# Low parts of the keys on both halves of the partitions: the second score pass on 128 rows instead of two times 64

## The chip, the cores and the metric

The kernel runs on one core of a Trainium2 chip. The metric is the device time of one execution in microseconds (us), as the median of several executions. The core's engines are named as the profile names them: PE (TensorE, matmul), PEld (its loading of the stationary operand), DVE (VectorE), ACT (ScalarE), POOL (GpSimd) and SP (SyncE). ACT and SP also issue the DMAs of this kernel, each from its own in-order queue.

## The reference, cut to what matters

One decoder layer on 1024 tokens of 1024 channels: a norm, one combined projection, an attention branch and a state space branch side by side, a gated sum of the two, an output projection, a norm and the residual. The change touches the attention branch alone, and of it the logits of the two softmax maps:

```python
q = q.reshape(b, s, ATT_HEADS, 2, ATT_QK_DIM)        # 8 heads, 2 maps, 64 channels
k = k.reshape(b, s, ATT_HEADS, 2, ATT_QK_DIM)
...
logits = jnp.einsum('bqhcd,bkhcd->bhcqk', q_i, k) * scale
logits = logits + bias[None, :, None]
logits = jnp.where(causal, logits, -jnp.inf)
p = jax.nn.softmax(logits, axis=-1)
a = p[:, :, 0] - lam * p[:, :, 1]
return jnp.einsum('bhqk,bkhe->bqhe', a, v)
```

## The kernel before

PE takes the operands in a 32-bit format that keeps fewer bits than float32, so each float32 value is held as the sum of a high part and a low part (`split`, L96), and a product of two such values is made in passes over PE that add up in one PSUM tile. A projection takes three passes per 128 rows of the contraction (`mm3`, L144: high by high, high by low, low by high).

The phases run one after the other: the norm and the transposed activations hTH and hTL, then eight heads of `attention(h)` (L253) with one `gates(h)` each, then `branch_att`, the state space branch, and the end. Inside a head:

- `proj_T` makes the queries (ps named pq) and keys (pk) of a head for 512 tokens at a time, channels on partitions: 24 matmuls of 512 columns each. The head has 2 x 64 channels, the two maps: map 0 on partitions 0 to 63 (`lo`), map 1 on 64 to 127 (`hi`).
- The queries go to qs. For map m, one half of the 128 partitions holds the high part of the queries and the other half the low part. So one pass over 128 rows against a key tile that holds the same 64 channels on both halves gives (high + low) times key.
- The keys' high part goes to kh in that doubled form: ACT writes each map on its own half (L274, L275), and two DMAs of 128 KB, issued from ACT's queue, copy it to the other half (L278, L279).
- The keys' low part, made by DVE (L276, L277), is held once: tile kl is [128, 1024], each map on its own half.
- `proj_N` makes values and output gates (ps named pv, 24 matmuls of 256 columns for each of 8 groups of tokens).
- `attend` (L310) then goes over eight blocks of 128 queries. For up to 512 keys at a time it makes the scores s of both maps in one tile of two PSUM banks: one pass per map over kh with 128 rows (L321), and one pass per map over kl with 64 rows (L323), which uses the rows 0 to 63 for map 0 and 64 to 127 for map 1. The key range is 256, 384 or 512 columns wide. DVE adds the bias near the diagonal (L328) and takes the maximum (L331), ACT takes the exponentials (L342), DVE combines the maps (L357, p), PE transposes p (L360, tile pta), ACT and DVE split it (L362 ah, L363 al), and PE multiplies by the values (L366, L367, tile po). Behind four blocks, the outputs are normed, gated and transposed (L305, tile pto).

The two passes of 64 rows:

```python
for m in range(2):
    nc.tensor.matmul(s[:, m, 0:wide], qs[:, m, qsl], kh[:, m, lo:lo + wide], start=True, stop=False)
for m in range(2):
    nc.tensor.matmul(s[:, m, 0:wide], qs[m * DK:(m + 1) * DK, m, qsl], kl[m * DK:(m + 1) * DK, lo:lo + wide], start=False, stop=True)
```

Every engine runs its own instructions in order. That order isn't that of the source: a scheduler lays it out when the program is built, from its own idea of what is ready when, and so weaves the projections of the next head, and the gates, between the steps of the blocks. A kernel with other instructions gets another order in that phase. The tiles qs, near, p, ah and al have two buffers; kh, kl, vv and gg have one, so a new head's keys are written only when the last score pass of the head before has read them. The PSUM pools have two buffers each: psp (pq, pk, pv, pg), pss (s, both banks) and pst (pta, po, pto).

## Time and profile before

| | us |
|---|---|
| median of 3 runs | 1942.09 |
| lowest and highest run | 1940.66, 1942.88 |
| span of the profiled execution | 1944.2 |
| PE busy in it | 1844.8 (95%) |
| DVE busy | 1181.2 (61%) |
| ACT busy | 863.2 (44%) |

The profiled execution's span is 2.1 us (0.1%) above the median of the runs; the profile gives no time around the span for this execution, so the sums are made against the span and carried over to the median as they are. A busy share is an average over phases with different limits. A PE record ends when the matmul's result is out, while the next one has long begun; what a matmul costs in a full stream is the distance from its start to the start of the next one, its slot, and the lines of time are read that way below.

### The profile page before, as it was taken

The numbers are of one execution on the slowest core, as the hardware profiler recorded it, in microseconds if no ns is written. First come the engines' busy times: TensorE is split into PE (matmuls) and PEld (weight loads), VectorE is DVE, ScalarE is ACT, GpSimd is POOL, SyncE is SP. The second block draws the span as 40 slices with busy tenths as digits, with TensorE's granted clock in tenths as the row PEclk, the third lists the DMA queues.
The fourth block names the chain that finished last, engine by engine and source line by source line (L and its number), as shares of the span: only waits on it lengthen the run. The fifth ranks groups of instructions, "written<-read, shape, count | busy, mean of one in ns | idle before, by whom it ended". The sixth has DMA issues, their size and how long they took to land. (4 is left out here: it accounts for less than half of the span.)

```text
span 1944.2 us, 27890 instructions
## 1 busy us (share of the span) xinstructions
PE 1844.8 (95%) x10249; PEld 1549.2 (80%) x10249; DVE 1181.2 (61%) x2782; ACT 863.2 (44%) x2135; POOL 136.3 (7%) x154
## 2 busy tenths in 40 slices
PE   6999999999999999999898989898989899999998
PEld 4888878788787878888787878787878777877786
DVE  5476575766758553347575767676767565545433
ACT  6454454544546342125445454545454444432221
POOL 1000000000000010001111111110101022000000
PEclk9999999999999999999999999999999999999999
DMA  6121121121111125513222222222222224753532
GB/s 197 45 68 55 42 58 49 53 60 53 49 47 55 33 90 197 159 49 81 63 66 65 66 66 67 70 64 68 65 71 62 65 49 146 233 178 137 177 109 70
DMA packets 219717, 165.14 MB, mean 85 GB/s; under 512 B 12220, under 2 KB 186654, under 8 KB 219582
## 3 DMA queue, kind: packets, MB, share of 16 engines
q1 hardware_dynamic: 169390, 117.21, 20.7%
q10 hardware_dynamic: 50192, 46.16, 8.2%
q8 instruction: 81, 1.33, 0.3%
q14 instruction: 54, 0.44, 0.1%
HBM read 129.63 MB, written 31.08 MB: 83 GB/s over the span
## 5 line engine op out<-in xcount | busy, mean ns | idle before, releaser
L150 PE MATMUL pz<-wzh,hTL 128*128 128x256 f32 (+1 forms) x512 | 151.4, 296 | 0.0
L150 PE MATMUL pz<-wzh,hTH 128*128 128x256 f32 (+1 forms) x512 | 149.1, 291 | 0.3 <-DVE dtr L539 0.3
L150 PE MATMUL pz<-wzl,hTH 128*128 128x256 f32 (+1 forms) x512 | 147.6, 288 | 0.0
L150 PE MATMUL pv<-wvl,hTH 128*128 128x256 f32 x512 | 145.3, 284 | 0.0
L150 PE MATMUL pv<-wvh,hTH 128*128 128x256 f32 x512 | 144.1, 281 | 0.3 <-DVE kl L277 0.3
L150 PE MATMUL pv<-wvh,hTL 128*128 128x256 f32 x512 | 144.3, 282 | 0.0
L586 ACT ACTIVATE mt<-mt,acs 128x128 f32<-128x128 f32 x256 | 85.5, 391 | 119.0 <-DMA mt<-arow_d 119.0
L331 DVE TENSOR_REDUCE ng<-s 128x2 f32<-128x1024 f32 (+2 forms) x96 | 90.9, 950 | 14.3 <-PE s L323 14.1
L580 POOL TENSOR_TENSOR v<-xb,dsk 128x256 f32<-128x256 f32 x64 | 51.2, 809 | 687.7 <-ACT xb L572 615.0
L150 PEld LDWEIGHTS pz<-wzh,hTH 128*128 128x128 f32 x512 | 97.1, 190 | 1.4 <-PE pz L150 0.5
L150 PEld LDWEIGHTS pv<-wvh,hTH 128*128 128x128 f32 x512 | 97.2, 190 | 1.2 <-PE pv L150 0.5
L150 PEld LDWEIGHTS pz<-wzl,hTH 128*128 128x128 f32 x512 | 97.0, 190 | 0.5
L150 PEld LDWEIGHTS pz<-wzh,hTL 128*128 128x128 f32 x512 | 96.7, 189 | 0.7
L150 PEld LDWEIGHTS pv<-wvl,hTH 128*128 128x128 f32 x512 | 97.0, 189 | 0.4
L150 PEld LDWEIGHTS pv<-wvh,hTL 128*128 128x128 f32 x512 | 96.2, 188 | 0.0
L513 DVE SCALAR_TENSOR_TENSOR xT<-ux,cw,xT 128x512 f32<-128x512 f32 x96 | 75.7, 789 | 21.3 <-ACT xT L511 19.9
L342 ACT ACTIVATE p<-s,ngm 128x512 f32<-128x512 f32 (+3 forms) x128 | 76.4, 609 | 25.6 <-DVE ngm L337 25.6
L607 PE MATMUL pd<-xdt,mt 128*128 128x64 f32 x512 | 66.6, 273 | 15.6 <-DVE st L605 9.6
L607 PEld LDWEIGHTS pd<-xdt,mt 128*128 128x128 f32 x512 | 62.4, 191 | 21.0 <-ACT mt L586 11.9
L288 DVE TENSOR_TENSOR vv<-pv,vv 128x128 fp32r<-128x128 f32 x64 | 18.7, 292 | 98.3 <-ACT vv L287 98.1
L366 PE MATMUL po<-vv,ah 128*128 128x256 f32 x288 | 74.7, 289 | 0.0
L367 PE MATMUL po<-vv,al 128*128 128x256 f32 x288 | 72.4, 284 | 0.0
(869 smaller groups left out, 5364.3 us busy)
## 6 DMA issues: line engine op xcount, KB each, us to landing
mt<-arow_d ACTq DMA_DIRECT2D x64, 256.0 KB, 5.3
sig_d<-gt ACTq DMA_DIRECT2D x32, 256.0 KB, 2.2
y_d<-yT ACTq DMA_DIRECT2D x32, 256.0 KB, 2.1
yT_l<-y_d SPq DMA_DIRECT2D x32, 256.0 KB, 5.2
xt<-in_x SPq DMA_DIRECT2D x8, 512.0 KB, 5.7
kh<-kh ACTq DMA_DIRECT2D x32, 128.0 KB, 2.3
o_d<-oT ACTq DMA_DIRECT2D x16, 256.0 KB, 2.0
oTl<-o_d SPq DMA_DIRECT2D x8, 512.0 KB, 6.2
```

Of the source, the lines that this page charges most:

```text
L150: nc.tensor.matmul(ps, a, b, start=(i == 0), stop=(i == n - 1))
L288: nc.vector.tensor_tensor(vv[:, t, DV:], ps[:, 0:DV], f32(vv[:, t, 0:DV]), op=ALU.subtract)
L331: nc.vector.tensor_reduce(ng, s[:, :, 0:width], axis=AX.X, op=ALU.max, negate=True)
L342: nc.scalar.activation(p[:, m, lo:lo + width], s[:, m, 0:width], AF.Exp, bias=neg[:, m:m + 1], accum_out=sums[:, i, m:m + 1])
L366: nc.tensor.matmul(po[:, 0:256], ah[:, k, :], vv[:, k, :], start=(k == 0), stop=False)
L367: nc.tensor.matmul(po[:, 0:256], al[:, k, :], vv[:, k, :], start=False, stop=(k == qb))
L513: nc.vector.scalar_tensor_tensor(out_h, u[:, j:j + 512], cw[:, j, ct:ct + 1], out_h, op0=ALU.mult, op1=ALU.add)
L580: nc.gpsimd.tensor_tensor(v4(v), v4(xb[:, 0:256]), b4(dsk[:, hs]), op=ALU.mult)
L586: nc.scalar.activation(mt[:, i, :], mt[:, i, :], AF.Relu, scale=-1.0, bias=acs[:, c, g * HG + i:g * HG + i + 1])
L607: nc.tensor.matmul(pd[:, 0, i * PH:(i + 1) * PH], mt[:, i, :], xdt[:, i * PH:(i + 1) * PH], start=True, stop=True)
```

## The change

The low part of the keys is now held like the high part, on both halves of the partitions. The tile kl becomes [128, 2, 1024], which adds 4 KB per partition to the pool of the attention phase. DVE writes each map on its own half as before, and two more DMAs of 128 KB per 512 tokens copy it to the other half, issued from ACT's queue behind those of kh. In `attend` the second pass of a map takes the same 128-row stationary operand qs as the first and kl with 128 rows; it follows its first pass directly, so the order of a group is kh and kl of map 0, then kh and kl of map 1. The product of the two low parts, which was left out before, is now in the sum. Comments and docstrings go too, which shifts nothing; lines L278 to L321 move down by one (the copies of kh are L279 and L280 now, the first pass L322), and from L323 on the numbers are those of before.

```diff
-        kl = work.tile([P, S], F32R, tag="kl", bufs=1, name=f"kl{h}")
+        kl = work.tile([P, 2, S], F32R, tag="kl", bufs=1, name=f"kl{h}")
...
-            nc.vector.tensor_tensor(kl[lo, sl], ps[lo], f32(kh[lo, 0, sl]), op=ALU.subtract)
-            nc.vector.tensor_tensor(kl[hi, sl], ps[hi], f32(kh[hi, 1, sl]), op=ALU.subtract)
-            nc.scalar.dma_start(f32(kh[hi, 0, sl]), f32(kh[lo, 0, sl]))
-            nc.scalar.dma_start(f32(kh[lo, 1, sl]), f32(kh[hi, 1, sl]))
+            nc.vector.tensor_tensor(kl[lo, 0, sl], ps[lo], f32(kh[lo, 0, sl]), op=ALU.subtract)
+            nc.vector.tensor_tensor(kl[hi, 1, sl], ps[hi], f32(kh[hi, 1, sl]), op=ALU.subtract)
+            for part in (kh, kl):
+                nc.scalar.dma_start(f32(part[hi, 0, sl]), f32(part[lo, 0, sl]))
+                nc.scalar.dma_start(f32(part[lo, 1, sl]), f32(part[hi, 1, sl]))
...
             for m in range(2):
                 nc.tensor.matmul(s[:, m, 0:wide], qs[:, m, qsl], kh[:, m, lo:lo + wide], start=True, stop=False)
-            for m in range(2):
-                nc.tensor.matmul(s[:, m, 0:wide], qs[m * DK:(m + 1) * DK, m, qsl], kl[m * DK:(m + 1) * DK, lo:lo + wide], start=False, stop=True)
+                nc.tensor.matmul(s[:, m, 0:wide], qs[:, m, qsl], kl[:, m, lo:lo + wide], start=False, stop=True)
```

The number of matmuls is the same, 192 passes over kh and 192 over kl; ACT gets 32 DMA issues more. The scheduler lays out the attention phase anew. From the last block of the last head on, the order of PE, DVE and ACT is the same as before, and on POOL and SP it is the same throughout. Three places show what moves.

PE, head 2 (counted from 0), block 2: the score passes of one tile s over 384 keys. L366 and L367 are of block 0's output, pg is of the gates. Before:

```order
1276 L321 MATMUL s_2_0_2621<-kh_2150,qs_2149 128x384
1277 L366 MATMUL po_0_2579<-vv_2152,ah_0_2572 128x256
1278 L321 MATMUL s_2_0_2621<-kh_2150,qs_2149 128x384
1279 L323 MATMUL s_2_0_2621<-kl_2151,qs_2149 128x384
1280 L367 MATMUL po_0_2579<-vv_2152,al_0_2573 128x256
1281 L323 MATMUL s_2_0_2621<-kl_2151,qs_2149 128x384
1282 L150 MATMUL pg_0_3016<-hTH,wm2h 128x512
```

The same tile in the changed kernel:

```order
1326 L322 MATMUL s_2_0_2633<-kh_2158,qs_2157 128x384
1327 L323 MATMUL s_2_0_2633<-kl_2159,qs_2157 128x384
1328 L322 MATMUL s_2_0_2633<-kh_2158,qs_2157 128x384
1329 L323 MATMUL s_2_0_2633<-kl_2159,qs_2157 128x384
1330 L150 MATMUL pg_0_3028<-hTL,wm2l 128x512
1331 L150 MATMUL pg_0_3028<-hTH,wm2h 128x512
```

Before, a full-array matmul stood between the two passes of 64 rows; now the four passes stand together, first and second pass of a map in turn. In the whole order before, 85 of the 96 pairs of 64-row passes stand next to each other and 11 are parted in this way (5 of 512 columns, 6 of 384).

ACT, head 2, blocks 6 and 7, where the keys of head 3 (ps pk_0) are read out of PSUM. Before:

```order
293 L274 ACTIVATE kh_3073<-pk_0_3129 64x512
294 L275 ACTIVATE kh_3073<-pk_0_3129 64x512
295 L278 DMA kh_3073<-kh_3073 64x512
296 L362 ACTIVATE ah_6_2875<-pta_6_0_2878 128x512
297 L362 ACTIVATE ah_6_2875<-pta_6_4_2886 128x384
298 L279 DMA kh_3073<-kh_3073 64x512
299 L342 ACTIVATE p_7_2929,sums_7_2930<-s_7_0_2912,ngm_7_2927 128x512 x2
300 L370 ACTIVATE sq_6_2908<-po_6_2892,rec_6_2871 128x128
301 L342 ACTIVATE p_7_2929,sums_7_2930<-s_7_512_2919,ngm_7_2927 128x512
302 L372 ACTIVATE sq_6_2908,sso_1_2724<-o_6_2907 128x128
303 L342 ACTIVATE p_7_2929,sums_7_2930<-s_7_512_2919,ngm_7_2927 128x512
```

In the changed kernel:

```order
311 L279 DMA kh_3085<-kh_3085 64x512
312 L280 DMA kh_3085<-kh_3085 64x512
313 L362 ACTIVATE ah_6_2887<-pta_6_0_2890 128x512
314 L362 ACTIVATE ah_6_2887<-pta_6_4_2898 128x384
315 L342 ACTIVATE p_7_2941,sums_7_2942<-s_7_0_2924,ngm_7_2939 128x512 x2
316 L370 ACTIVATE sq_6_2920<-po_6_2904,rec_6_2883 128x128
317 L342 ACTIVATE p_7_2941,sums_7_2942<-s_7_512_2931,ngm_7_2939 128x512
318 L372 ACTIVATE sq_6_2920,sso_1_2736<-o_6_2919 128x128
319 L342 ACTIVATE p_7_2941,sums_7_2942<-s_7_512_2931,ngm_7_2939 128x512
320 L279 DMA kl_3086<-kl_3086 64x512
321 L280 DMA kl_3086<-kl_3086 64x512
322 L269 ACTIVATE qs_3084<-pq_1_3174 64x512
```

The two new DMA issues stand behind the exponentials of block 7, and ahead of the reading of the next queries.

PE, head 1, block 7: the end of block 6's output (po) and the transposes of block 7 (pta). The matmuls pq_1 are the next head's queries. Before:

```order
1012 L366 MATMUL po_6_1969<-vv_1229,ah_6_1952 128x256
1013 L367 MATMUL po_6_1969<-vv_1229,al_6_1953 128x256
1014 L150 MATMUL pq_1_2237<-hTH,w_2l 128x512
1015 L150 MATMUL pq_1_2237<-hTH,w_2h 128x512
1016 L150 MATMUL pq_1_2237<-hTL,w_2h 128x512
1017 L150 MATMUL pq_1_2237<-hTH,w_2l 128x512
```

In the changed kernel:

```order
1057 L366 MATMUL po_6_1977<-vv_1233,ah_6_1960 128x256
1058 L367 MATMUL po_6_1977<-vv_1233,al_6_1961 128x256
1059 L360 MATMUL pta_7_0_2028<-cst,p_7_2014 128x128 x4
1060 L150 MATMUL pq_1_2247<-hTL,w_2h 128x512
1061 L150 MATMUL pq_1_2247<-hTH,w_2l 128x512
1062 L360 MATMUL pta_7_4_2036<-cst,p_7_2014 128x128 x4
```

Before, 18 matmuls of 512 columns stood between po_6 and pta_7; now pta_7 follows po_6 directly. Counted from the end of block 7's scores to its first transpose, 32 matmuls of 512 columns, 7 transposes and 14 matmuls of 256 columns stood between before, and 22, 7 and 14 now, and the same in heads 3 and 5 of the changed kernel; in the other heads between 24 and 33 of 512 columns stand there, before and now.

## Rows read from the trace of the kernel before

**Rows 1.** The head of the page and its first part: the span; busy time, share of the span and instructions of each engine.

```profile
span 1944.2 us, 27890 instructions
PE 1844.8 (95%) x10249; PEld 1549.2 (80%) x10249; DVE 1181.2 (61%) x2782; ACT 863.2 (44%) x2135; POOL 136.3 (7%) x154
```

**Rows 2.** Busy time of each engine in one stretch, from the first score pass to the end of the last head's scores: us; busy us (instructions) of PE, PEld, DVE, ACT, POOL; granted clock of PE as a share of full speed; DMA share; GB/s.

```profile
57.00:703.00 646.00, 641.09 (x3882) 531.99 (x3881) 419.07 (x1070) 318.07 (x944) 23.21 (x18) 1.00 0.18 51
```

**Rows 3.** Who waited for whom in that stretch, PE alone: us in total, times, longest.

```profile
PE pta L360 <- DVE p L357: 2.4, 3, 0.9
PE pto L305 <- DVE o L304: 2.2, 8, 0.4
```

**Rows 4.** Instructions of PE in order of time, a group of 512 columns and the projection behind it: start us, duration us, engine, line, operation, out<-in, rows*columns of the array, count (two records that overlap are merged to one).

```profile
283.59 0.62 PE L321 MATMUL s<-kh,qs 128*128 128x512 f32 x2
284.14 0.50 PE L323 MATMUL s<-kl,qs 64*128 64x512 f32 x2
284.57 0.50 PE L150 MATMUL pk<-hTL,w_3h 128*128 128x512 f32 x1
284.90 0.39 PE L150 MATMUL pk<-hTH,w_3l 128*128 128x512 f32 x1
285.13 0.40 PE L150 MATMUL pk<-hTH,w_3h 128*128 128x512 f32 x1
285.37 0.39 PE L150 MATMUL pk<-hTL,w_3h 128*128 128x512 f32 x1
285.60 0.40 PE L150 MATMUL pk<-hTH,w_3l 128*128 128x512 f32 x1
```

**Rows 5.** The same view, two groups of 256 columns one behind the other, with the matmuls around them.

```profile
140.18 0.28 PE L150 MATMUL pv<-wvh,hTL 128*128 128x256 f32 x1
140.30 0.40 PE L321 MATMUL s<-kh,qs 128*128 128x256 f32 x2
140.63 0.38 PE L323 MATMUL s<-kl,qs 64*128 64x256 f32 x2
140.94 0.50 PE L321 MATMUL s<-kh,qs 128*128 128x256 f32 x2
141.37 0.38 PE L323 MATMUL s<-kl,qs 64*128 64x256 f32 x2
141.69 0.39 PE L150 MATMUL pv<-wvh,hTH 128*128 128x256 f32 x1
141.91 0.28 PE L150 MATMUL pv<-wvl,hTH 128*128 128x256 f32 x1
```

**Rows 6.** The same view, a group of 384 columns whose pair stands together.

```profile
81.80 0.51 PE L321 MATMUL s<-kh,qs 128*128 128x384 f32 x2
82.24 0.44 PE L323 MATMUL s<-kl,qs 64*128 64x384 f32 x2
82.61 0.50 PE L150 MATMUL pg<-hTH,wm0l 128*128 128x512 f32 x1
82.95 0.39 PE L321 MATMUL s<-kh,qs 128*128 128x512 f32 x1
```

**Rows 7.** The same view, a group of 384 columns whose pair is parted: the place in head 2, block 2, of which the order stands above.

```profile
245.61 0.34 PE L321 MATMUL s<-kh,qs 128*128 128x384 f32 x1
245.88 0.44 PE L323 MATMUL s<-kl,qs 64*128 64x384 f32 x1
246.25 0.38 PE L367 MATMUL po<-vv,al 128*128 128x256 f32 x1
246.56 0.44 PE L323 MATMUL s<-kl,qs 64*128 64x384 f32 x1
246.93 0.50 PE L150 MATMUL pg<-hTH,wm2h 128*128 128x512 f32 x1
247.26 0.39 PE L150 MATMUL pg<-hTL,wm2h 128*128 128x512 f32 x1
```

**Rows 8.** Groups of instructions by line and shape: the 64-row passes; count, busy us, mean ns of one, idle time of PE just before them.

```profile
L323 PE MATMUL s<-kl,qs 64*128 64x512 f32 x96 | 26.4, 495 | 0.0
...
L323 PE MATMUL s<-kl,qs 64*128 64x256 f32 x64 | 12.3, 381 | 0.0
...
L323 PE MATMUL s<-kl,qs 64*128 64x384 f32 x32 | 9.7, 437 | 0.0
```

**Rows 9.** Line L279 alone, the second copy of kh: time of the issue on ACT's queue (ns: min/median/max), first and last start; and the time from issue to landing.

```profile
L279 ACTq DMA_DIRECT2D kh<-kh x16: 468/508/553, 41.3 to 638.6; - x16
...
DMA to landing us min/median/max: 2.2/2.3/3.7
```

**Rows 10.** Instructions of ACT in order of time, around the first keys of head 1: the last issue of the copies of kh.

```profile
121.16 0.50 ACTq L279 DMA_DIRECT2D kh<-kh  x1
```

**Rows 11.** Instructions of DVE in order of time, at the same place: the last write of the low parts kl.

```profile
123.25 0.69 DVE L277 TENSOR_TENSOR kl<-pk,kh 64x512 fp32r<-64x512 f32 x1
```

**Rows 12.** Instructions of PE in order of time, block 7 of head 3: its last 64-row pair and its first transposes.

```profile
368.13 0.50 PE L323 MATMUL s<-kl,qs 64*128 64x512 f32 x2
...
377.15 0.63 PE L360 MATMUL pta<-cst,p 128*128 128x128 f32 x4
```

**Rows 13.** Instructions of DVE in order of time, the same block: the first and the last step between those two.

```profile
368.68 0.70 DVE L328 TENSOR_TENSOR s<-s,near 128x512 f32<-128x512 f32 x1 [0.26 <-PE s L323]
...
376.25 0.75 DVE L357 SCALAR_TENSOR_TENSOR p<-p,nlam 128x512 f32<-128x512 f32 x1
```

## Prediction

> **What bounds the kernel now.** I read the page's first part, then the stretch in which the changed lines run, then the lines of time inside it. PE is busy for 95% of the span [rows 1]. Between 57 and 703 us, where all score passes run, it is busy for 641.1 of 646.0 us at full granted clock, with DVE at 419 and ACT at 318 [rows 2], and the waits that PE is charged with there are a few microseconds [rows 3]. So in this phase the kernel takes as long as PE's stream of matmuls is, and a microsecond taken off that stream is a microsecond of the kernel, as long as the softmax steps on DVE and ACT come in time. A busy share doesn't say whether the stream itself is dense; the starts do. In a plain stream a matmul of 512 columns starts 0.23 us after the last one (284.90 to 285.60 in three steps [rows 4]), one of 256 columns 0.12 us (140.18 to 140.30 [rows 5]); for 384 columns I take the middle, 0.175 us. These are the slots I count with.
>
> **Part 1, the 64-row pairs go.** A pair of 64-row passes does run side by side: two records of mean 495 ns [rows 8] cover 0.50 us together [rows 4]. But the starts around it show what it costs. Of 512 columns: from the first L321 at 283.59 to the second matmul behind the pair at 284.90 there are 1.31 us, in which two full passes and one projection matmul have 3 x 0.232 = 0.70; so the pair costs 0.61. Part of it lies in itself (284.14 to 284.57), part ahead of it and part in the next matmul, whose slot is 0.33 and not 0.23 [rows 4]. Two full 128-row passes cost 0.46: a saving of 0.15 each. Of 256 columns: 140.30 to 141.91 is 1.61 us for two pairs, four full passes and one projection matmul; less 5 x 0.118 that is 1.02, or 0.51 a pair, against 0.24: a saving of 0.27 [rows 5]. Of 384: 81.80 to 82.95 is 1.15, less 2 x 0.175 + 0.23 leaves 0.57 against 0.35: 0.22 [rows 6]. Where another matmul parts the pair, the price is paid twice: 245.61 to 247.26 is 1.65, less 0.175 + 0.12 + 0.23 leaves 1.12 against 0.35: 0.77 [rows 7].
> There are 48 pairs of 512, 32 of 256 and 16 of 384 columns (half of each count in [rows 8]), and the order parts 5 of 512 and 6 of 384. So 43 x 0.15 + 32 x 0.27 + 10 x 0.22 + 11 x 0.77 = 6.5 + 8.6 + 2.2 + 8.5 = **25.8 us** less. This is the largest term, and it holds if a pass over kl with 128 rows costs a slot like the pass over kh.
> Against this stands a rule: the Trainium skill, TensorEngine Tiling (Array Packing), section Overview, gives a contraction of 64 or less up to twice the speed when two such matmuls share the array; its section Tiling Modes adds that a change of the mode drains the engine. The trace agrees that the two share the array, and that the stream pays around them; by the first rule alone the change would lose what the rival "the pair was one pass" below works out.
>
> **Part 2, the new copies.** Two DMAs more for each of 16 half-heads. Their landing: a copy of kh lands 2.3 us (at most 3.7) after its issue [rows 9]. In head 1 the last low part is ready at 123.94 [rows 11], 2.3 us after the last issue of kh's copies ended [rows 10], so kl lands some 3 to 5 us behind kh. In the new order the first pass over kl stands 17 us of slots or more behind the projection of the first keys of its head (head 1: 17.4), so I cost the landing at 0. It would cost up to 2 us a head if the order left less than about 8.
> Their issue: 0.5 us each on ACT [rows 9], 32 of them, 16 us on an engine that is idle for half of the stretch [rows 2]. ACT waits there until DVE has written kl; behind it stand the reading of the next queries (L269) and, in the blocks, the split of the transposes (L362). Both ends: 0, where ACT would have waited anyway for the transposes, and 16 us, where each issue delays PE in full. I take 2 us, near the low end, since the transposes come behind DVE steps that the issue doesn't delay. DVE's own work stays as it was.
>
> **Part 3, the new order.** The handoffs from softmax to PE are where a shorter stream gives time back. Block 7 is the longest: in head 3 its scores end at 368.6 and its first transpose starts at 377.15, right behind the first half of p (377.0) [rows 12, 13]: the chain takes 8.4 us. In the new order heads 1, 3 and 5 have 22 x 0.232 + 7 x 0.12 + 14 x 0.12 = 7.6 us of slots there (0.12 for a transpose is an upper estimate: four together take 0.63 us [rows 12]), so PE waits about 1 us, or 3 where DVE and ACT have other work in between. The other heads have 8.0 to 9.3, where before there were 8.2 to 10.1. Nothing below 0 is to be expected in these three heads; elsewhere a reshuffle can also take away waits, of which there are a few now [rows 3]. Bounds: -3 and +10 us over the phase; I take **+4**.
> The wider kl takes 4 KB more per partition of a pool that ends with the phase: 0. From the last head's last block on the order is unchanged, so what follows just starts earlier: 0.
>
> **The sum.** 1944.2 - 25.8 + 0 + 2 + 4 = 1924.4 us for the profiled execution; the median of the runs is 2.1 us lower, so **1922 us**, 1.0% faster. Ends: 25.8 plus 3 of waits that go gives 1913; 25.8 less 10 and less a third of ACT's 16 gives about 1932.
>
> **The rivals.**
> *The handoffs take most of it.* PE is dense now because the stream is long enough to hide the softmax chains. If the other five heads wait as the three do, with 2 to 3 us in a head at two blocks, 12 to 16 us come back on top: 1934 to 1938. For it: the chain of block 7 had no room to spare in head 3 [rows 12, 13]. Against it: PE's waits on p are 2.4 us in all now, in three places [rows 3], and the other blocks' room is about as before.
> *The cost stays.* If the gaps around the pair come from the change of the key tile and not from the 64 rows, the new passes cost a full slot plus the same gaps: ahead of and behind the pair about 0.2 us are lost, and the pair's own stretch (0.43 for 512, 0.31 for 256) becomes 0.46 and 0.24. That gains about 1 us for the pairs that stand together and 4 for the parted ones, less 6 of parts 2 and 3: 1943, no change. Against it: L366 and L367 change operands at every step.
> *The pair was one pass.* If two 64-row passes cost the time of one, doubling it adds a slot per pair: 48 x 0.232 + 32 x 0.118 + 16 x 0.175 = 17.7 us, 1960. It is what a packed array suggests; the starts in [rows 4 to 6] speak against it.
> *ACT's queue becomes the bound (slower).* At 16 places ACT holds two issues, and waits for DVE's second kl before that; in head 1 that write came 1.5 us after the issues of kh were through [rows 10, 11]. With its 0.69 us and two issues that is up to 3.2 us in which exponentials and splits stand still. If all of it reaches PE: 16 x 3.2 = 51 us, less 26: 1967. It decides for slower from 26 / 16 = 1.6 us per half-head on. Against it: the scheduler put the issues behind the exponentials in heads 3, 5 and 7, and ACT idles half the time [rows 2].
>
> **How the numbers follow.** The forecast, PE's stream shrinks by what the pairs cost and some of it goes into waits, 1912 to 1932: 80%. Handoffs take most, 1932 to 1939: 9%. The cost stays, 1939 to 1945: 4%. ACT's queue: 5% (1946 and more); one pass: 2% (1960). The range of 8 in 10 reaches a little into the second case: **1911 to 1935**. About 0.2% (4 us) is what a measurement of this kernel can tell from no change; faster by more than that 89%, within 4%, slower 7%.
>
> **What would show it.** In the profile after: passes over kl with 128 rows that start 0.23, 0.175 and 0.12 us after the pass over kh, and the matmul behind a group in a normal slot, show part 1. Score passes that wait for a DMA of kl would show part 2 wrong. Waits of PE for p (L357) of 1 to 3 us ahead of block 7's transposes in heads 1, 3 and 5, in total some 4 us more than now, show part 3. ACT idle ahead of the new issues, followed by PE waiting for L342 or L362, would show the last rival. The phase from the first to the last score pass should end near 683 where it ends near 703 now. The prediction is wrong if the kl slots are longer than the kh slots, or if PE's waits in the phase rise by more than 10 us.

## The result, and the profile after

The changed kernel takes **1930.6 us** in the median of 4 runs (1928.73 to 1933.76), the kernel before beside it on the same chip 1942.49 us (4 runs, 1940.66 to 1946.22): a ratio of 0.9936, interval 0.9917 to 0.9954. It is faster by 11.9 us, where 20 were forecast. One execution of one kernel below, e_gdve, ran at a mean granted clock of 0.70 and is left out.

The head of the page after and the stretch from the first to the last score pass, to hold against [rows 1, 2]:

```profile
span 1929.4 us, 27946 instructions
PE 1828.1 (95%) x10249; PEld 1564.5 (81%) x10249; DVE 1183.5 (61%) x2782; ACT 862.4 (45%) x2135; POOL 136.3 (7%) x154
```

```profile
57.00:690.00 633.00, 619.61 (x3868) 543.68 (x3868) 417.66 (x1064) 316.12 (x943) 23.16 (x18) 0.99 0.21 59
```

PE's busy time in the phase fell by 21.5 us, from 641.1 to 619.6, but the phase shrank by 13 only: 13.4 of 633 us are idle now, where 4.9 of 646 were. The granted clock is no longer 1.00 throughout. Both are new.

The first matmul of the state space phase (tile pz) is the cleanest mark in the traces: what stands ahead of it holds all that the change touches. Before and after, PE in order of time:

```profile
832.15 0.30 PE L150 MATMUL pz<-wzh,hTH 128*128 128x288 f32 x1
```

```profile
821.53 0.30 PE L150 MATMUL pz<-wzh,hTH 128*128 128x288 f32 x1
```

So 10.6 us are won by there. The rest of the difference between two executions is not the change's: from that matmul to the first one of the output projection of that branch (tile pys) there are 825.4 us before and 819.2 after, with the same instructions in the same order, and from 813 to 825 us in the kernels below that keep that order. I compare kernels by this mark, and give the whole times beside it. Each mark is of one traced execution, and it also holds what moves ahead of the phase: the first score pass starts between 56.2 and 58.4 us in all kernels but e_zero (44.9) and e_plmem (54.6), so a microsecond or two of a difference can lie there. From the first to the last score pass there are 643.0 us before and 632.8 after, 10.2 less.

**The passes.** A group of 512 columns and the projection behind it, as in [rows 4], and the start of a group of 256 columns, as in [rows 5]:

```profile
279.38 0.39 PE L322 MATMUL s<-kh,qs 128*128 128x512 f32 x1
279.61 0.39 PE L323 MATMUL s<-kl,qs 128*128 128x512 f32 x1
279.85 0.39 PE L322 MATMUL s<-kh,qs 128*128 128x512 f32 x1
280.07 0.40 PE L323 MATMUL s<-kl,qs 128*128 128x512 f32 x1
280.31 0.40 PE L150 MATMUL pk<-hTL,w_3h 128*128 128x512 f32 x1
280.55 0.39 PE L150 MATMUL pk<-hTH,w_3l 128*128 128x512 f32 x1
```

```profile
138.70 0.28 PE L322 MATMUL s<-kh,qs 128*128 128x256 f32 x1
138.82 0.40 PE L323 MATMUL s<-kl,qs 128*128 128x256 f32 x2
```

Every start is one slot behind the last, 0.23 and 0.12 us, and the projection behind the group too; over the whole trace a pass over kl starts 0.232, 0.179 and 0.118 us (median) behind its pass over kh, for 512, 384 and 256 columns. The four passes and the matmul behind them take 280.55 - 279.38 = 1.17 us, where [rows 4] had 1.31 for the same work. This part came as forecast.

**The waits.** PE's waits up to the end of the last scores (57 to 692 us), as in [rows 3]:

```profile
PE pto L306 <- DVE o L305: 11.3, 8, 2.6
PE pta L360 <- DVE p L357: 1.3, 2, 0.8
```

The wait for p went down (2.4 to 1.3 us), the wait for o went from 2.2 to 11.3 us. Three of its eight places make most of it: heads 1, 3 and 5, at 212.19, 376.02 and 539.85 us. PE at the first of them, in order of time:

```profile
212.19 0.40 PE L150 MATMUL pk<-hTH,w_2h 128*128 128x512 f32 x1
215.15 0.30 PE L306 MATMUL pto<-cst,o 128*128 128x128 f32 x1 [2.57 <-DVE o L305]
...
217.13 0.63 PE L150 MATMUL pk<-hTL,w_2h 128*128 128x512 f32 x1
217.56 0.63 PE L150 MATMUL pk<-hTH,w_2l 128*128 128x512 f32 x1
...
218.82 0.39 PE L150 MATMUL pk<-hTH,w_2l 128*128 128x512 f32 x1
```

The same place before:

```profile
218.79 0.39 PE L150 MATMUL pk<-hTL,w_2h 128*128 128x512 f32 x1
219.41 0.50 PE L305 MATMUL pto<-cst,o 128*128 128x128 f32 x2 [0.23 <-DVE o L304]
```

Two losses follow each other. The slot ahead of pto is 2.96 us, against 0.62 before. Then matmuls of 512 columns start 0.43 us apart, not 0.23, until 218.82. Busy time by stretch (the columns of [rows 2]) shows why:

```profile
212.20:215.20 3.00, 0.43 (x3) 0.08 (x2) 2.81 (x9) 0.00 (x0) 0.37 (x1) 1.00 0.62 166
215.20:218.60 3.40, 3.40 (x11) 2.68 (x12) 0.59 (x3) 0.69 (x1) 0.00 (x0) 0.53 0.03 11
```

The granted clock is 0.53 in the 3.4 us behind the gap: the lower of its two levels, 1.2 instead of 2.4 GHz, for nearly all of it; in the next 3.4 us it is 0.97. It costs 3.4 x (1 - 0.53) = 1.6 us. The other two places read alike (0.53 and 0.54). So 3 x (2.96 - 0.62 + 1.6) = 11.8 us went there.

**Why o is late.** DVE at the first place. Between the sum of squares and o stand eleven small steps of the rsqrt (L115, L105, three times L107 to L109), of 0.16 us each:

```profile
208.96 0.17 DVE L115 TENSOR_SCALAR rsv_o<-sso 128x4 f32<-128x4 f32 x1 [0.47 <-ACT sq L372]
...
209.76 1.15 DVE L109 SCALAR_TENSOR_TENSOR rsy_o<-rst_o,rsy_o 128x4 f32<-128x4 f32 x1
...
211.34 1.25 DVE L109 SCALAR_TENSOR_TENSOR rsy_o<-rst_o,rsy_o 128x4 f32<-128x4 f32 x1
...
212.82 0.69 DVE L271 SCALAR_TENSOR_TENSOR qs<-pq,qs 64x512 fp32r<-64x512 f32 x1
...
213.73 0.69 DVE L272 SCALAR_TENSOR_TENSOR qs<-pq,qs 64x512 fp32r<-64x512 f32 x1
...
214.65 1.14 DVE L305 SCALAR_TENSOR_TENSOR o<-o,rsy_o,gg 128x128 f32<-128x128 f32 x4
```

The first step and o at the same place before:

```profile
216.73 0.17 DVE L115 TENSOR_SCALAR rsv_o<-sso 128x4 f32<-128x4 f32 x1 [0.47 <-ACT sq L372]
...
218.91 0.88 DVE L304 SCALAR_TENSOR_TENSOR o<-o,rsy_o,gg 128x128 f32<-128x128 f32 x3
```

From the first step to o there are 214.65 - 208.96 = 5.69 us; before it was 2.18. 1.4 us are the low parts of the next queries (L271, L272), which now stand among the steps. The other 2.1 are two small steps that took 1.15 and 1.25 us. At those times POOL, which splits the gates' weights, runs:

```profile
209.58 1.31 POOL L99 TENSOR_TENSOR wm2l<-wm2r,wm2h 128x512 fp32r<-128x512 f32 x1 [77.55 <-DVE rst_o L107]
211.27 1.30 POOL L99 TENSOR_TENSOR wm2l<-wm2r,wm2h 128x512 fp32r<-128x512 f32 x1 [0.38 <-ACT wm2h L98]
```

209.76 + 1.15 = 210.91 and 209.58 + 1.31 = 210.89; 211.34 + 1.25 = 212.59 and 211.27 + 1.30 = 212.57: each long step ends with POOL's instruction.

The Trainium skill, SBUF — State Buffer, section SBUF: two separate sides, calls the port pair that DVE and GpSimd share an exclusive lock: where a DVE step has two inputs in SBUF and a GpSimd instruction reads SBUF, whichever starts first has the pair for its whole instruction, and the other waits. The trace agrees, with these two pairs of ends: both steps read two tiles in SBUF. It shows the other side as well. Of the DVE steps that start while POOL subtracts or multiplies, those with one operand in PSUM take their usual time (qs<-pq, 4 of 4; v<-pd,v of the state space phase, 19 of 19), and those with both in SBUF are held until POOL is done (rsy_o<-rst_o,rsy_o, 7 of 7; xdt<-xb,dts of the state space phase, 24 of 24).

### The profile page after: what moved, and what is told of

It is laid out like the page before. It is cut to its first block, busy times and chain, and to the rows that moved or that the text cites. A ratio compares the mean times of both kernels' runs of the same rounds, so it can differ in the third digit from the quotient of the medians.

```text
span 1929.4 us, 27946 instructions
## 1 busy us (share of the span) xinstructions
PE 1828.1 (95%) x10249; PEld 1564.5 (81%) x10249; DVE 1183.5 (61%) x2782; ACT 862.4 (45%) x2135; POOL 136.3 (7%) x154
## 5 line engine op out<-in xcount | busy, mean ns | idle before, releaser
L331 DVE TENSOR_REDUCE ng<-s 128x2 f32<-128x1024 f32 (+2 forms) x96 | 91.3, 952 | 12.4 <-PE s L323 11.9
L366 PE MATMUL po<-vv,ah 128*128 128x256 f32 x288 | 74.8, 289 | 0.0
L367 PE MATMUL po<-vv,al 128*128 128x256 f32 x288 | 71.8, 282 | 0.0
```

The source lines that it names most:

```text
L331: nc.vector.tensor_reduce(ng, s[:, :, 0:width], axis=AX.X, op=ALU.max, negate=True)
L366: nc.tensor.matmul(po[:, 0:256], ah[:, k, :], vv[:, k, :], start=(k == 0), stop=False)
L367: nc.tensor.matmul(po[:, 0:256], al[:, k, :], vv[:, k, :], start=False, stop=(k == qb))
```

## The experiments

My theory: the passes save what was forecast, and the new order of the scheduler (the planner, below), which ACT's new DMAs bring about, puts o late in three heads. Its rivals: the DMAs themselves cost; any shorter stream of PE is given back at the handoffs; and, within the theory, that POOL's overlap alone makes the gap, or the steps of the queries alone. All twelve, with the kernel before and the change; the third column is the start of the first pz, the last PE's wait at pto from 57 to 700 us (total, longest; where the stream is shorter, this takes in one wait of 0.2 us from behind the last scores):

| kernel | median us | ratio to before [interval] | pz | wait at pto |
|---|---|---|---|---|
| before | 1942.49 | | 832.1 | 2.2, 0.4 |
| changed | 1930.60 | 0.9936 [0.9917, 0.9954] | 821.5 | 11.3, 2.6 |
| e_zero | 1923.44 | 0.9884 [0.9848, 0.9920] | 816.8 | 4.9, 2.4 |
| e_poolq | 1920.70 | 0.9882 [0.9848, 0.9916] | 808.9 | 3.0, 1.0 |
| e_bcopies | 1947.99 | 1.0020 [1.0001, 1.0039] | 836.3 | 10.8, 2.6 |
| e_grouped | 1931.06 | 0.9947 [0.9925, 0.9969] | 821.5 | 11.3, 2.6 |
| e_plmem | 1907.66 | 0.9826 [0.9808, 0.9845] | 805.4 | 5.2, 1.3 |
| e_gdve | 1911.74 | 0.9847 [0.9825, 0.9870] | | |
| e_gdve_again | 1911.57 | 0.9842 [0.9823, 0.9861] | 806.1 | 2.4, 0.4 |
| e_bpermap | 1990.65 | 1.0258 [1.0236, 1.0280] | 880.2 | 1.8, 0.3 |
| e_spq | 1920.06 | 0.9898 [0.9878, 0.9917] | 809.0 | 3.0, 1.0 |
| e_bgdve | 1932.80 | 0.9944 [0.9926, 0.9961] | 826.2 | 1.8, 0.5 |
| e_spq_gdve | 1913.28 | 0.9845 [0.9827, 0.9862] | 804.7 | 1.7, 0.5 |
| e_pool4 | 1926.76 | 0.9927 [0.9903, 0.9951] | 810.9 | 7.8, 1.5 |

### Without the order: the copies on another queue, or none

**e_poolq**, and later **e_spq** with `nc.sync` in the place of `nc.gpsimd`:

```diff
-            for part in (kh, kl):
-                nc.scalar.dma_start(f32(part[hi, 0, sl]), f32(part[lo, 0, sl]))
-                nc.scalar.dma_start(f32(part[lo, 1, sl]), f32(part[hi, 1, sl]))
+            for part, eng in ((kh, nc.scalar), (kl, nc.gpsimd)):
+                eng.dma_start(f32(part[hi, 0, sl]), f32(part[lo, 0, sl]))
+                eng.dma_start(f32(part[lo, 1, sl]), f32(part[hi, 1, sl]))
```

> The changed kernel with the copies of kl given by POOL's queue; those of kh stay with ScalarE. The computation is whole. The planner's order has no qs and no kl step among the rsqrt steps. Theory (order): 1917 to 1919, no gap of 2.6 us at pto. Rival (the copies' transfers cost, whoever gives them): 1928 to 1931. Rival (shorter TensorE work is given back at the handoffs anyway): about 1930.

> The changed kernel with the copies of kl given by SP's queue instead of ScalarE; everything is computed, and the order on the engines is that of the kernel whose kl copies POOL gave. Theory (the order of the rsqrt steps, set off by ScalarE's extra DMAs, is what the changed kernel lost): as there, no gap of 2.6 us at pto, 1918 to 1922, the first to last score pass at 620 us. Rival (POOL's giving of the DMAs happened to move POOL's splits out of the way): gaps at pto again, 1926 to 1931.

Both came as the theory has it, e_poolq 1.7 us above its range in the whole time: pz at 808.9 and 809.0 us, 23 us ahead of the kernel before and 12.5 ahead of the changed one, with every DMA still made. The planner gave both the order of the kernel before up to pz, instruction by instruction, on DVE and ACT, and on PE but for the score passes. The waits of e_spq, from 57 to 700 us:

```profile
PE pta L360 <- DVE p L357: 3.1, 4, 0.9
PE pto L306 <- DVE o L305: 3.0, 9, 1.0
```

The gaps are gone, and with them the lower clock (1.00 from 57 to 677 us). That the DMAs' transfers cost, and that the gain is given back in any case, are both out. What PE gives back at handoffs with the shorter stream is about 3 us: 23.1 of 26.

How ACT's issues led to it is seen in ACT's rows at the first place, the changed kernel first (the first issue of kl's copies, the sums of squares, L372, and behind them the high parts of the gates' weights, L98), then e_spq:

```profile
204.31 0.47 ACTq L279 DMA_DIRECT2D kl<-kl  x1
...
208.52 0.31 ACT L372 ACTIVATE sq<-o 128x128 f32<-128x128 f32 x1 [0.42 <-DVE o L371]
...
208.83 0.62 ACT L98 ACTIVATE wm2h<-wm2r 128x512 fp32r<-128x512 f32 x1
...
210.56 0.63 ACT L98 ACTIVATE wm2h<-wm2r 128x512 fp32r<-128x512 f32 x1
```

```profile
204.58 0.63 ACT L98 ACTIVATE wm2h<-wm2r 128x512 fp32r<-128x512 f32 x1 [2.15 <-PE pq L150]
...
207.29 0.63 ACT L98 ACTIVATE wm2h<-wm2r 128x512 fp32r<-128x512 f32 x1
...
209.47 0.31 ACT L372 ACTIVATE sq<-o 128x128 f32<-128x128 f32 x1 [0.42 <-DVE o L371]
```

POOL's split follows each L98. In e_spq both are done before the sums of squares are ready; in the changed kernel both come behind them, and so POOL runs just when DVE is at the rsqrt.

**e_zero**: no copies of kl at all. One tile for all heads, the other half of each map set to zero once:

```diff
+        kl = work.tile([P, 2, S], F32R, tag="kl", bufs=1, name="kl")
+        nc.vector.memset(f32(kl[64:128, 0, :]), 0.0)
+        nc.vector.memset(f32(kl[0:64, 1, :]), 0.0)
...
-            for part in (kh, kl):
-                nc.scalar.dma_start(f32(part[hi, 0, sl]), f32(part[lo, 0, sl]))
-                nc.scalar.dma_start(f32(part[lo, 1, sl]), f32(part[hi, 1, sl]))
+            nc.scalar.dma_start(f32(kh[hi, 0, sl]), f32(kh[lo, 0, sl]))
+            nc.scalar.dma_start(f32(kh[lo, 1, sl]), f32(kh[hi, 1, sl]))
```

> The changed kernel without the copies of the low parts: the second pass takes kl with 128 rows, but the other half of each map is zeroed once at the start and stays zero (so the product of low part with low part is left out, as in the kernel before). ScalarE gives no more DMAs than in the kernel before, and the planner returns to an order in which neither the qs step nor the kl step stands between the steps of an output block's rsqrt. Theory (the order costs some 14 us: three gaps of 2.6 us at pto and half the clock behind each): 24 to 26 us below the kernel before, about 1917 to 1919, no gap over 2 us at pto in heads 1, 3 and 5. Rival (whatever is faster on TensorE is given back at the handoffs): about 1930, like the changed kernel, with the gaps elsewhere. Rival (the DMAs cost): 1917 to 1919 here, but the kernel with the copies on another queue stays at 1925 to 1930.

Only half hit: pz at 816.8, 15.3 us ahead of before, not 24 to 26. My reading of its order was wrong for the start of the phase: its first score pass comes at 44.9 us, not 56.8, and PE waits there; and in the first head the queries' steps and two long small steps do stand in the rsqrt (5.55 us to o). The wait at the start:

```profile
PE s L320 <- DVE qs L270: 5.3, 1, 5.3
```

No gap stands in heads 1, 3 and 5. It is one more order with its own luck, and says little about copies.

### The order alone, and the passes alone

**e_bcopies**: the kernel before with the changed kernel's tile, copies and order, and still its 64-row passes.

```diff
-                nc.tensor.matmul(s[:, m, 0:wide], qs[:, m, qsl], kl[:, m, lo:lo + wide], start=False, stop=True)
+            for m in range(2):
+                nc.tensor.matmul(s[:, m, 0:wide], qs[m * DK:(m + 1) * DK, m, qsl], kl[m * DK:(m + 1) * DK, m, lo:lo + wide], start=False, stop=True)
```

> The kernel before, its pairs of 64 rows kept, with kl made as two maps and copied to the other half as in the change, the copies being read by nobody. It has the changed kernel's order of instructions on every engine, and its DMAs. Theory (order): the three gaps at pto in heads 1, 3 and 5 come here too, at up to 2.6 us each, with half the clock behind them: about 1953 to 1956. Since the stream of TensorE is longer by 0.77 us per pair here, part of a gap may be covered: down to 1947. Rival (the gaps come of the shorter TensorE work and not of the order): 1942 to 1944.

The three gaps came with the order, each 2.96 us from start to start as in the changed kernel, so they don't come of the shorter stream. But the kernel lost less than I expected: 4.2 us at pz, below my 5 to 14. Part of the reason is the clock. Behind the first gap and the second:

```profile
220.60:224.00 3.40, 3.40 (x22) 3.00 (x23) 0.59 (x3) 1.58 (x3) 0.00 (x0) 1.00 0.20 77
...
387.00:390.40 3.40, 3.40 (x11) 2.66 (x12) 0.59 (x3) 0.69 (x1) 0.00 (x0) 0.51 0.00 0
```

The same gap of 2.96 us is followed by full clock at the first place (and the third) and by half clock at the second. Three gaps, one fall of the clock and the smaller gap in head 6 (1.68 us) come to 3 x 2.34 + 1.6 + 1.06 = 9.7 us; 5.5 of it are given back elsewhere in this order: 1.6 by shorter waits for p (0.8 us, against 2.4 in [rows 3]), and about 2.6, by the prediction's prices, because it parts 7 of the pairs (1 of 512 columns, 3 of 384, 3 of 256) where the order before parts 11: (5 - 1) x 0.62 + (6 - 3) x 0.55 - 3 x 0.50. Where the rest lies I did not follow up.

With e_spq this makes a table of four, the pz mark: old order with 64 rows 832.1, old order with 128 rows 809.0, new order with 64 rows 836.3, new order with 128 rows 821.5. The passes are worth 23.1 us in the old order and 14.8 in the new; the order costs 4.2 us with the long passes and 12.5 with the short. The two parts don't simply add up, since the order also sets how many pairs are parted and where PE waits.

**e_bgdve** and **e_spq_gdve**: the same pair once more in a third order. In both, DVE makes the gates' splits; the second has the change with kl's copies from SP.

```diff
-        wg = load_cols(w_in, 0, OM + d * P, P, "wa", f"wm{d}", eng=nc.gpsimd)
+        wg = load_cols(w_in, 0, OM + d * P, P, "wa", f"wm{d}")
```

> Control: the kernel before with the gates' low parts worked out by VectorE instead of POOL; nothing of the change. Its order on TensorE and VectorE is that of the next kernel (two kl steps stand in the rsqrt of heads 1, 3 and 5). Theory (POOL's splits cost the kernel before little, since none of them met an rsqrt there): 1935 to 1943, and the state-space phase starts within 3 us of where it does in the kernel before, 832.1 us. Rival (POOL's splits hold up VectorE enough to matter with the long passes too): 1920 to 1930.

> The changed kernel with the copies of kl given by SP's queue and the gates' low parts worked out by VectorE; everything is computed. It differs from the control in the passes and the copies alone, so the difference of the two is what the passes are worth with no change of order: theory 21 to 26 us below the control by the start of the state-space phase (26.2 us of pairs removed, up to 5 us given back at handoffs). As a whole: 1908 to 1918, no half clock between 60 and 690 us. Rival (VectorE, busier by 0.7 us per split, becomes the one waited for): 1920 to 1928, PE's waits for p and o above 8 us together.

804.7 against 826.2: the passes are worth 21.5 us here, with the same order on DVE, ACT and POOL; 1.8 of it lie ahead of the first score pass (58.4 and 56.6 us), and from the first to the last pass it is 19.5, where e_spq has 22.6. This order parts only 5 pairs, all of 512 columns, so the prediction's prices give 22.5 for it; the 26.2 of the expectation holds for the old order at most.

The control gained 5.9 us by itself, more than the theory had (3) and less than the rival. Part of it is that order: 6 pairs of 384 columns fewer are parted, 3.3 us by the prediction's prices. Part is POOL, which held DVE up in the kernel before as well. DVE at head 3 of that kernel, two halves of p that take 0.75 us each when alone [rows 13], and POOL beside them:

```profile
293.94 2.47 DVE L357 SCALAR_TENSOR_TENSOR p<-p,nlam 128x512 f32<-128x512 f32 x2
```

```profile
294.58 1.28 POOL L99 TENSOR_TENSOR wm3l<-wm3r,wm3h 128x512 fp32r<-128x512 f32 x1 [78.47 <-ACT wm3h L98]
```

The second half is held for about 1 us, and PE waits 0.86 us for it; head 6 has the same. These are two of the three waits for p in [rows 3], and the control has none. The 5.9 us are not taken apart further.

**e_grouped** puts the second passes behind both first ones:

```diff
                 nc.tensor.matmul(s[:, m, 0:wide], qs[:, m, qsl], kh[:, m, lo:lo + wide], start=True, stop=False)
+            for m in range(2):
                 nc.tensor.matmul(s[:, m, 0:wide], qs[:, m, qsl], kl[:, m, lo:lo + wide], start=False, stop=True)
```

> The changed kernel with the passes of a block's scores in the order kh map 0, kh map 1, kl map 0, kl map 1 instead of map by map; all of 128 rows, the order on all other engines as in the change. If the gain of the passes is the row count alone: the same as the changed kernel, 1928 to 1933. If it is the change of the written bank that costs a part (each pass here goes to the other map's bank than the one ahead of it): slower by up to 85 times 0.1 us, 1939.

pz at 821.5, the same to 0.1 us: the map order, and with it the bank written, is worth nothing. The row count is all.

**e_bpermap** parts every pair of the kernel before:

```diff
             for m in range(2):
                 nc.tensor.matmul(s[:, m, 0:wide], qs[:, m, qsl], kh[:, m, lo:lo + wide], start=True, stop=False)
-            for m in range(2):
                 nc.tensor.matmul(s[:, m, 0:wide], qs[m * DK:(m + 1) * DK, m, qsl], kl[m * DK:(m + 1) * DK, m, lo:lo + wide], start=False, stop=True)
```

> The kernel before with its score passes map by map: kh map 0, kl map 0 (64 rows), kh map 1, kl map 1 (64 rows), so that no two passes of 64 rows follow each other; the copies are made as in the change and read by nobody, the order elsewhere is that of the kernel before. If a pass of 64 rows between passes of 128 costs as much as the parted pair of the kernel before did (start to start 0.77 us above two normal slots for 512 columns, where a pair together costs 0.31 us): 85 half-block pairs at some 0.5 us more, about 40 us, 1975 to 1995. If only the row groups' overlap was lost, and the change of the row count costs nothing: each pair at two normal slots, below the kernel before, 1915 to 1925.

pz at 880.2, 48.1 us later than before. The prediction's prices give 43 x (0.77 - 0.15) + 32 x (0.77 - 0.27) + 10 x (0.77 - 0.22) = 48.2 for it. Its rows show the toll, from start to start, PE in order of time:

```profile
100.97 0.39 PE L321 MATMUL s<-kh,qs 128*128 128x512 f32 x1
101.29 0.49 PE L322 MATMUL s<-kl,qs 64*128 64x512 f32 x1
101.71 0.50 PE L321 MATMUL s<-kh,qs 128*128 128x512 f32 x1
102.14 0.49 PE L322 MATMUL s<-kl,qs 64*128 64x512 f32 x1
102.56 0.39 PE L321 MATMUL s<-kh,qs 128*128 128x256 f32 x1
```

Four passes of 512 columns take 1.59 us (100.97 to 102.56), each 0.32 to 0.43 from the next, where four slots are 0.93 and the kernel before with its pair together needs 0.98 (283.59 to 284.57 in [rows 4]): 0.61 more, where the price is 0.62. (The 0.77 that the expectation gives for 512 columns is that of the parted pair of 384 in [rows 7].) Every change between 128 and 64 rows costs, and the pair of the kernel before had paid it once.

### What makes the gap: the queries' steps, or POOL

**e_gdve** (the line of e_bgdve, on the changed kernel) and **e_plmem**:

```diff
-        (eng or nc.vector).tensor_tensor(l, src, f32(h), op=ALU.subtract)
+        if eng is None:
+            nc.vector.tensor_tensor(l, src, f32(h), op=ALU.subtract)
+        else:
+            eng.memset(f32(l), 0.0)
```

> The changed kernel with the gates' low parts worked out by VectorE instead of POOL. The planner then puts two of these steps of some 0.7 us and the two qs steps into the rsqrt of heads 2, 4 and 6, and one split into that of head 0. Theory (whatever stands in the rsqrt delays o, and PE waits at pto): the way to o takes 2.18 + 4 x 0.7 = 5.0 us there, gaps of 1.5 to 2 us in heads 2, 4 and 6 and none in 1, 3 and 5, and about 1924 to 1929. Rival (POOL's work beside VectorE is what makes the gap): no gap over 1 us, and 1917 to 1921.

> The same kernel as the one with the gates' low parts on VectorE, once more for its trace, which was taken in an execution at a granted clock of 0.70. Theory (whatever stands in the rsqrt delays o): 1910 to 1915, the way to o 4.7 us in heads 2, 4 and 6 and PE waiting there for 1 to 2 us. Rival (without POOL beside VectorE the rsqrt is early enough): no wait over 0.5 us at pto.

> The changed kernel in which POOL fills the low part of the gates' weights with zero instead of working it out from two operands (so the gates lose the product with that low part; TensorE takes as many matmuls as before). Around the output blocks' rsqrt the order is that of the changed kernel: in heads 1, 3 and 5 the two qs steps still stand in it. In the changed kernel the way from the first of the rsqrt steps to o takes 5.70 us there, against 2.18 us where it is alone: 1.4 us are the two qs steps and some 2.1 us two small steps of 1.15 and 1.25 us beside POOL's work. Theory (both parts make the gap): if the fill doesn't stop VectorE, the way falls to 3.6 us, PE's wait at pto from 2.57 us to about 0.5 us, no half clock behind it, and the time to 1920 to 1924. Rival (the qs steps alone make the gap, POOL's overlap is chance): the small steps stay at over 1 us or the gap stays over 2 us, 1928 to 1931. If the fill stops VectorE as the subtraction does, the same 1928 to 1931, with a small step as long as what is left of the fill.

The edit of e_plmem reaches further than its expectation says: the weights of the state space phase, whose low parts VectorE works out, are filled with zero too, and so are the first head's low parts on POOL. Its whole time and its mark can't be held against the others; what follows reads heads 1, 3 and 5 alone.

Here my theory gave way to its rival, and both e_gdve (1911.74) and e_plmem (1907.66) came out below every range given for them. In e_gdve_again the way to o is 4.61 us in heads 2, 4 and 6, from two splits and two queries' steps between the rsqrt steps, longer than e_plmem's; yet PE waits 0.3 us:

```profile
295.05 0.50 PE L306 MATMUL pto<-cst,o 128*128 128x128 f32 x2 [0.32 <-DVE o L305]
```

In its order the planner leaves room for these steps and puts pto later: PE's last matmul ahead of it starts 4.40 us behind the first rsqrt step (294.34 against 289.94), in heads 1, 3 and 5 of the changed kernel 3.23 us (212.19 against 208.96), before 2.06. What its order leaves no room for is a small step that stands still for POOL. In the changed kernel the two stalls are 1.15 + 1.25 - 2 x 0.16 = 2.08 us; without them pto would come 0.88 us behind that matmul, near the 0.62 of before. In e_plmem POOL's fill still stalls one step:

```profile
205.88 1.03 DVE L118 TENSOR_SCALAR rsv_o<-sso 128x4 f32<-128x4 f32 x1 [0.47 <-ACT sq L375]
```

0.86 us above its 0.17; the way to o is 4.47 us and the slot at pto 1.74 = 0.88 + 0.86. No lower clock follows. The step that the fill held has one operand. Steps with two, which the subtraction holds, run at their usual 0.16 us beside a fill, here in head 7, POOL first:

```profile
614.84 0.99 POOL L102 MEMSET wm8l<- 128x512 f32 x2 [7.47 <-issue]
```

```profile
615.11 0.16 DVE L111 SCALAR_TENSOR_TENSOR rst_o<-rst_o,rsv_o 128x4 f32<-128x4 f32 x1
615.30 0.16 DVE L112 SCALAR_TENSOR_TENSOR rsy_o<-rst_o,rsy_o 128x4 f32<-128x4 f32 x1
```

So what counts is not that POOL is busy, but what its instruction and the DVE step read.

**e_pool4** leaves POOL's work whole and cuts each instruction in four:

```diff
-        (eng or nc.vector).tensor_tensor(l, src, f32(h), op=ALU.subtract)
+        if eng is None:
+            nc.vector.tensor_tensor(l, src, f32(h), op=ALU.subtract)
+            return
+        for k in range(4):
+            eng.tensor_tensor(l[:, k], src[:, k], f32(h)[:, k], op=ALU.subtract)
```

> The changed kernel with each of POOL's subtractions for the gates' low parts (512 columns, 1.30 us) given as four of 128 columns; everything is computed, and up to the state-space phase TensorE and VectorE have the changed kernel's order. In the changed kernel a small step of the rsqrt (0.16 us) that starts beside a subtraction ends with it: 209.76 + 1.15 is 210.91 us and the subtraction's 209.58 + 1.31 is 210.89; 211.34 + 1.25 and 211.27 + 1.30 likewise. With that, the way to o is 5.70 us in heads 1, 3 and 5, of which 2.07 us are these two stalls, and PE's slot at pto is 2.96 us. Theory (a small step waits for the end of the one POOL instruction that runs): the stalls are up to 0.35 us each, some 0.7 to 1.4 us together, the way to o 4.3 to 5.0 us, the slot 1.6 to 2.3 us, the time 1922 to 1927. Rival (VectorE waits till POOL has nothing more to do): the stalls stay at 1.15 and 1.25 us or grow, the slot at 2.9 us or more, 1928 to 1933. Rival (POOL's stalls are not what makes the gap): the stalls shrink and the slot stays.

The stalls became small and many, as the theory has it. DVE in head 1:

```profile
209.69 0.39 DVE L111 TENSOR_TENSOR rst_o<-rsy_o 128x4 f32<-128x4 f32 x1
210.11 0.38 DVE L112 SCALAR_TENSOR_TENSOR rst_o<-rst_o,rsv_o 128x4 f32<-128x4 f32 x1
```

The way to o is 4.66 us, the slot at pto 1.93, and the clock stays at 1.00 in all three places. pz comes at 810.9, 10.6 us earlier than in the changed kernel. From the first to the last score pass it is 8.5 us; the three places give 3 x (2.96 - 1.93 + 1.6) = 7.9. Of the whole time 4 us are seen (1926.76; 1919.98 to 1928.77), and the intervals of the two ratios overlap; the edit also cuts VectorE's own low parts of the state space phase in four, which adds 6.5 us to DVE's busy time.

The fastest kernels that compute everything are e_gdve (0.9842 [0.9823, 0.9861] in its second set of runs) and e_spq_gdve (0.9845 [0.9827, 0.9862]): some 30 us below the kernel before, and some 18 below the change as it stands.

## Why the prediction was right, and where it was not

- **What bounds the kernel**: right. A microsecond off PE's stream is one of the kernel, where the order holds: 23.1 us at the mark in e_spq, of 25.8 taken off.
- **Part 1, 25.8 us**: right in mechanism and size. The kl slots are those of the forecast (0.232, 0.179 and 0.118 us in the median); 23.1 and 21.5 us net in two orders that are the same on both sides, where the prices give 25.8 and 22.5; 48.1 us where the same prices forecast 48.2 for the opposite edit. *The pair was one pass* and *the cost stays* are out by this.
- **Part 2, landing 0**: right; no wait for kl's copies stands in the list. **Issue 2 us**: the mechanism was wrong. No wait of PE for ACT stands in its list, and the transfers cost nothing from another queue. But the prediction wrote that "DVE's own work stays as it was", and this step failed: the two issues that stand ahead of L269 and L98 in ACT's queue changed what the planner put where, and brought POOL's splits and the rsqrt together. With the copies on SP's queue the mark comes 12.5 us earlier.
- **Part 3, +4 us**: the sign was right, the place wrong. Block 7's p is in time: in head 3 the last pass starts at 358.43 and the first transposes of p at 366.36, 7.9 us later, where there were 9.0 in [rows 12]; the chain is no fixed length, as I had taken it. PE's wait for p fell to 1.3 us. The wait came at pto instead, for o, which the prediction had looked at only as 2.2 us in [rows 3]: +9.1 us. All waits together rose by 8.5 us (4.9 of 646 to 13.4 of 633), within the bound of +10; with the fall of the clock behind the gaps, some 4.8 us for three places, which was in no term, the loss is 13.3, above it and more than three times the +4 of the sum.
- **The sum**: 20 us forecast, 11.9 measured, 10.6 by the mark: 25.8 less 11.8 at the three places, less 1.06 and 1.17 at two smaller gaps (slots of 1.68 and 1.40 us at 626.92 and 672.56, before 0.62 and 0.23), is 11.8; I did not trace the last microsecond. The phase should have ended near 683 us and ended at 689.5, 10.7 us ahead of the 700.2 of before. That 1930.6 lies inside the range of 1911 to 1935 owes something to luck: the range was wide enough for a loss that the sum had neither the place nor the cause of.
- **The rivals**: *handoffs take most* (1934 to 1938) comes near in size, but not in the cause: with the old order the handoffs take back 3 us, and with the new one most of the loss is at three places that POOL's splits and the order make. *ACT's queue becomes the bound* did not happen.

What stays open: the last microsecond of the sum and the rest of e_bcopies and of the control, as said above; and why the same gap of PE is followed by the lower clock at some places and not at others.

## What to carry to other kernels

Price a narrow matmul by the starts around it, not by its record: here a pair of 64-row passes ran together in 0.50 us and still cost more than two full passes. And where a planner makes the order, look at what an added DMA issue moves on its engine (12.5 us here, where PE waited for no issue): keep work of POOL that reads SBUF away from a short chain of DVE steps with both operands in SBUF that PE waits for, or give it to DVE, where the planner's order leaves room for it.

## What the runs showed that I had not expected

- A DVE step of 0.16 us took up to 1.25 us beside a subtraction of POOL, ending with it each time; with the POOL instruction a quarter as wide it took 0.39. A fill by POOL stalled a step of one operand (1.03 us) and no step of two; a subtraction stalled no step with an operand in PSUM.
- A gap of 2.96 us from start to start on PE was followed by the lower clock in the changed kernel and in e_grouped at three places of three, in e_bcopies at one of three (0.51 against 1.00 and 1.00); a gap of 2.79 us in e_zero was not, nor were those of e_pool4 and e_plmem (1.93 and 1.74 us in head 1) at any of three places each.
